# A two-layer DeltaNet and Conformer trunk: order of splits, filling, norm steps, scalar turns and first w_out columns

## The chip, the cores and the metric

One core of one Trainium2 chip runs the whole program. The metric is the device time of one execution in microseconds (us). Before the change three runs gave a median of 3172.94 us (3172.18 to 3173.76).

## What is computed

Two layers over 2048 tokens of width 1024, all in float32. Each layer normalises x, projects it, and has two branches: a gated DeltaNet (4 heads of 128, chunked scans forward and backward, summed) and a Conformer convolution (width 31, layer norm over 512 channels). Each branch is projected to 1024, the two are merged by sigmoid gates, and `w_out` follows.

```python
proj = h @ w_in                                   # 5648 columns: qkv, z_a, a, b, cf_val, cf_glu, z_b, gates
qkv = silu(depthwise_conv_centred(qkv, conv_w))   # width 5
g = -exp(a_log) * softplus(a_lg + dt_bias); beta = sigmoid(b_lg)
o = gated_delta_chunked(q, k, v, g[:, :, 0], beta[:, :, 0]) + flip(gated_delta_chunked(flipped inputs))
o = o * rsqrt(mean(o * o) + EPS) * dn_norm_w * silu(z_a);  y_a = o @ w_dn_out
u = depthwise_conv_centred(cf_val * sigmoid(cf_glu), cf_conv_w) + cf_conv_b
u = silu(layer_norm(u, cf_ln_w, cf_ln_b));                  y_b = (u * silu(z_b)) @ w_cf_out
gate = sigmoid(gate_lg + gate_b)
x = x + (gate[:, :, 0] * y_a + gate[:, :, 1] * y_b) @ w_out  # after the last layer: rms_norm
```

## The kernel before

Everything is kept channel by token, in 8 tiles of 128 channels; tokens come in halves of 1024 and blocks of 512. A float32 product is made of three matmuls: both operands are split into a high part (rounded to float32r by ScalarE, L158) and a low part (the difference, by VectorE, L159), and `dense_steps` (L170 to L178) issues high x high (L175), high x low (L176) and low x high (L177) for each 128 rows k of the contraction. A tile of one column of 128 outputs by 512 tokens is 24 matmuls for k = 8, or 12 for k = 4. `weight` (L161) loads a column of weights through SP and splits it; `whi`, `wlo` and `wraw` have two buffers each, `st` tiles three, `pd` banks of PSUM three and `pz` banks five.

The order of the work comes from generators. In the projections `dense` (L180) calls `follow` (one step of each of the queued head tasks in `post`) and `pump` (the background tasks in `back`) after each tile of matmuls; a background task yields its cost in us, and a yield of 0.0 ends this turn, so that the next step comes a tile later. `conformer_norm` (L749) is such a task for each of four blocks: mean (L766), squares and their token sum by `token_sum` (L201), reciprocal root on VectorE, `spread` over the channels (L212 on VectorE, L214 on TensorE), scale, SiLU, store of u on POOL's queue. The string `Z` says how many zero yields stand between the steps. `scalar_tiles` (L404) makes the 16 columns of decay and write strength per block (L414, L415), copies them (L417, into the `st` tile `ab`) and transposes them (L420); `scalars` (L424) is the first task in `post`, with the cumulative sums (L472 to L474). `conv_tiles` (L512) calls the block's scalar turn ahead of the block's two columns, and `step_lead` moves the norm of the coming block on.

`delta` (L818) is the scan: 16 steps, in each a forward and a backward chunk. All instructions from its start to the end of the filling are bound to the written order on TensorE, ScalarE, VectorE and GpSimd by `bind`. In a step, for both directions: products of k and of q with the state (L973, L976), `prep` of the coming chunks (L920 to L956), the inverse (L989), new state and output (L998, L1007), and `finish` of a pair of chunks: squares on ScalarE (L1028), reciprocal root on VectorE, scale on ScalarE (L1046), transposes (L1051) into `pz` and the product with the gate on VectorE (L1052), which is stored to `og` on SP. In between `pull(n)` takes n pieces of other TensorE work, a piece being the three matmuls of one k. LEAD says how many ahead of the first step, STEP how many at four places of each step, and TAIL how many ahead of each of the last five parts, of the last two pairs:

```python
            next(new)            # step: squares of the pair just finished
            pull(STEP[2])
            next(last)           # transposes of the pair before it
            ready = go(step + 1)
            last = new
            pull(STEP[3])
...
        for n, part in zip(TAIL, (new, last, new, new, new)):
            pull(n)
            next(part)
        for _ in fill:
            pass
        self.bind(start)
```

The pieces come from `filler` (L1135): 256 of `gates(1)`, then 64 of `early_merge` (L1171), which is the product of `w_cf` with u for the first half: 16 groups of four pieces, each with a sigmoid (L1181) at its start, a weight split at every other start, and the eviction y (L1187) at its end. u's eight splits are emitted when piece n of SPLITS has been taken and the next one is asked for.

`merge` (L1208) then does `w_dn` and (for the second half) `w_cf` for eight columns j, with gate loads and sigmoids (L1239), products (L1247, L1253, L1254), split into `yhi`, `ylo`; then the eight columns of `w_out`. In the last layer `last_out` (L1313) does this by blocks of 512 with a closing norm (`close`: token sums L206, spread, eight multiplies L1346, stores). Outside of the scan the scheduler of the tile framework places ready instructions by the order in which they were emitted.

Of the kernel before, what the change touches and what calls it, by code (L numbers as in the profile page):

```python
# [19 lines left out]
KD = 8  # L20
# [5 lines left out]
R1 = 3.0  # L26
R3 = 4.5
GAP = 0
SPLITS = (245, 247, 249, 251, 253, 255, 257, 258)
LEAD = (8, 10, 6, 6, 6, 4)  # L30
STEP = (4, 4, 4, 4)
TAIL = (2, 2, 1, 3, 4)
Z = '121'
PART = 5
LATE = 4
# [27 lines left out]
def cut(x):  # L63
    return x.rearrange("p (a i) -> p a i", a=2)
# [13 lines left out]
class Trunk:  # L78
# [325 lines left out]
    def scalar_tiles(self):  # L404
        nc = self.nc
        w = self.wab
        pt = self.pz()

        def block(blk):
            xs = self.hx(blk)  # L410
            ps = self.pd()
            for k in range(KD):
                xhi, xlo = (mix(x) for x in xs(k))
                nc.tensor.matmul(ps, w[:, k, :], xhi, start=k == 0, stop=False)  # L414
                nc.tensor.matmul(ps, w[:, k, :], xlo, start=False, stop=k == KD - 1)  # L415
            ab = self.st("ab")
            nc.scalar.activation(cut(ab[0:32, :]), sort(ps[0:32, :]), AF.Copy)  # L417
            for i in range(4):
                c = 4 * blk + i
                nc.tensor.transpose(pt[:, c * 32:(c + 1) * 32], ab[0:32, i * P:(i + 1) * P], self.ident[0:32, 0:32])  # L420

        return block, pt

    def scalars(self, pt):  # L424
        nc, l, a = self.nc, self.l, self.a
# [39 lines left out]
        v_.tensor_scalar(out=n(9), in0=n(9), scalar1=1.0, scalar2=None, op0=ALU.add)  # L465
        v_.reciprocal(out=n(9), in_=n(9))
        v_.tensor_copy(dch(self.beta), cdh(n(9)))
        yield
        ps = self.pz()
        tri = self.st("tri")[:, 0:256].rearrange("p (d c) -> p d c", d=2)  # L470
# [41 lines left out]
    def conv_tiles(self, cols, block=None):  # L512
        nc = self.nc
        self.rate = R1
        ws = [self.weight(self.a["w_in"][self.l, c], KD) for c in cols]
        accs = []
        prev = [None] * len(cols)
        for half in range(2):
            cur = []
            for i, c in enumerate(cols):  # L520
                cur.append(self.padded(half, TAPS, prev[i], "cin") if half or not i else None)
            for b in range(2):
                blk = 2 * half + b
                self.need(blk)
                if block:
                    self.step_lead(2)
                    block(blk)
                for i, c in enumerate(cols):
                    self.step_lead(2)
                    ps = self.pd()  # L530
                    self.dense(ps, ws[i], self.hx(blk), KD)
                    if cur[i] is None:
                        cur[i] = self.padded(half, TAPS, prev[i], "cin")
                    t, o = cur[i]
                    nc.scalar.activation(cut(t[:, o + b * NB:o + (b + 1) * NB]), sort(ps), AF.Copy)  # L535
            if half == 0 and self.l:
                self.need(2)
            for i, c in enumerate(cols):
                t, o = cur[i]
                prev[i] = t  # L540
                if half == 0:
                    accs.append(self.mid("acc"))
                n = HALF - 2 if half == 0 else HALF + 2
                out = accs[i][:, 0:n] if half == 0 else accs[i][:, HALF - 2:L]
                self.conv(out, t, n, TAPS, V_CONV + c * TAPS, 0.0)
                nc.scalar.activation(out, out, AF.Silu)
        self.rate = R2
        return accs
# [200 lines left out]
    def conformer_norm(self, blk):  # L749
        nc = self.nc  # L750
        v_ = nc.vector
        sl = slice(blk * NB, (blk + 1) * NB)
        cv = self.mid("lnc")[:, 0:L].rearrange("p (j t) -> p j t", t=NB)
        self.load(cv, self.cv_d[:, :, sl].rearrange("j p t -> p j t"))
        zb = self.mid("lnz")[:, 0:L].rearrange("p (j t) -> p j t", t=NB)
        self.load(zb, self.zb_d[:, :, sl].rearrange("j p t -> p j t"))
        t = self.st("lnt")
        s2 = self.st("lns")
        v_.tensor_tensor(out=t, in0=cv[:, 0, :], in1=cv[:, 1, :], op=ALU.add)
        v_.tensor_tensor(out=s2, in0=cv[:, 2, :], in1=cv[:, 3, :], op=ALU.add)  # L760
        v_.tensor_tensor(out=t, in0=t, in1=s2, op=ALU.add)
        yield 1.8
        for _ in range(int(Z[0])):
            yield 0.0
        ps = self.pz()
        nc.tensor.matmul(ps, self.ones, t, start=True, stop=True)  # L766
        v_.scalar_tensor_tensor(out=cv, in0=ps[:, None, :].to_broadcast([P, 4, NB]), scalar=-1.0 / 512,
                                in1=cv, op0=ALU.mult, op1=ALU.add)
        nc.scalar.activation(t, cv[:, 0, :], AF.Square)
        for j in range(1, 4):  # L770
            nc.scalar.activation(s2, cv[:, j, :], AF.Square)
            v_.tensor_tensor(out=t, in0=t, in1=s2, op=ALU.add)
        yield 4.0
        for _ in range(int(Z[1]) + (blk == 3)):
            yield 0.0
        pt = self.pz()
        self.token_sum(pt, t, 4)
        vv = self.sm(4, "lv")
        r = self.sm(4, "lr")
        v_.tensor_scalar(out=vv, in0=pt[:, 0:4], scalar1=1.0 / 512, scalar2=EPS, op0=ALU.mult, op1=ALU.add)  # L780
        self.rsqrt(r, vv, 4)
        yield 1.5
        for _ in range(int(Z[2])):
            yield 0.0
        pr = self.pz()
        self.spread(pr, r, 4)
        v_.tensor_tensor(out=cv, in0=cv, in1=pr[:, None, :].to_broadcast([P, 4, NB]), op=ALU.mult)
        yield 2.6
        for j in range(4):
            nc.scalar.activation(cv[:, j, :], cv[:, j, :], AF.Silu, scale=self.vec[:, V_LW + j:V_LW + j + 1],  # L790
                                 bias=self.vec[:, V_LATE + j:V_LATE + j + 1])
        v_.tensor_tensor(out=cv, in0=cv, in1=zb, op=ALU.mult)
        self.pstore(self.u_d[:, :, sl].rearrange("j p t -> p j t"), cv)
# [414 lines left out]
    def merge(self, l, xd, fnw):  # L1208
# [10 lines left out]
        for half in range(2):  # L1219
# [10 lines left out]
            for j in range(KD):  # L1230
                ys = {}
                wc = self.weight(a["w_cf"][l, j], 4) if half else None
                wd = self.weight(a["w_dn"][l, j], 4)
                for b in order:
                    tk = slice(half * HALF + b * NB, half * HALF + (b + 1) * NB)
                    gt = self.hm("gt")[:, 0:2 * NB].rearrange("p (n t) -> p n t", n=2)
                    n = 1 + half
                    self.load(gt[:, 0:n], self.gt_d.rearrange("(n j) p t -> j p n t", n=2)[j][:, 0:n, tk])
                    nc.scalar.activation(gt[:, 0:n], gt[:, 0:n], AF.Sigmoid)  # L1239
                    ys[b] = [gt[:, 0, :], gt[:, 1, :] if half else self.y1[:, j, b * NB:(b + 1) * NB]]  # L1240
                if half:
                    for b in order:
                        sl = slice(b * NB, (b + 1) * NB)
                        y = ys[b]
                        ps = self.pd()
                        self.dense(ps, wc, lambda k: (u[:, k, sl], u[:, 4 + k, sl]), 4)
                        v_.tensor_tensor(out=cut(y[1]), in0=sort(ps), in1=cut(y[1]), op=ALU.mult)  # L1247
                for b in order:
                    sl = slice(b * NB, (b + 1) * NB)
                    y = ys[b]  # L1250
                    ps = self.pd()
                    self.dense(ps, wd, lambda k: (og[:, k, sl], og[:, 4 + k, sl]), 4)
                    v_.tensor_tensor(out=cut(y[0]), in0=sort(ps), in1=cut(y[0]), op=ALU.mult)  # L1253
                    v_.tensor_tensor(out=y[0], in0=y[0], in1=y[1], op=ALU.add)  # L1254
                    self.split(yhi[:, j, sl], ylo[:, j, sl], y[0])
# [3 lines left out]
                og, pg = self.operands(self.og_d, 1, "gop")  # L1259
                ahead = (f(k) for f in (pu, pg) for k in range(4))  # L1260
            if last:
                self.last_out(l, half, xd, fnw, yhi, ylo, ahead, order)
                continue
            w = self.weight(a["w_out"][l, 0], KD)
            norm = self.normalise(0, *prev, wcol) if prev is not None else iter(())
            xn = []
            for j in range(KD):
# [42 lines left out]
        yield  # L1310
        yield from self.normalise(1, xn, r, wcol)

    def last_out(self, l, half, xd, fnw, yhi, ylo, ahead, order):  # L1313
        nc, a = self.nc, self.a
        v_ = nc.vector

# [39 lines left out]
        for b in order:  # L1356
# [1 line left out]
            xn = [t[:, i * NB:(i + 1) * NB] for t in (self.mid("xl"), self.mid("xl")) for i in range(4)]  # L1358
            ss = self.hm("ss")[:, 0:NB]
            whole = PART if half and b else KD  # L1360
            w = self.weight(a["w_out"][l, 0], KD)
            if whole < KD:
                hold = self.big([P, 2, KD, NB], F32R, "wend").rearrange("p a b c -> p (a b c)")
                parts = [hold[:, i * D:(i + 1) * D].rearrange("p (k c) -> p k c", c=P) for i in range(2 * (KD - whole))]
# [7 lines left out]
            for j in range(whole):  # L1372
# [7 lines left out]
                if whole < KD and j and len(ws) < KD - whole:  # L1380
# [2 lines left out]
                        self.split(hi[:, k:k + 4, :], lo[:, k:k + 4, :], raws[len(ws)][:, k:k + 4, :])  # L1383
                    ws.append((hi, lo))
            if whole == KD:
                run(close(o, NB, None))
                continue
            start = self.mark()
# [80 lines left out]
```

## Time and profile before

| | |
|---|---|
| median of 3 runs | 3172.94 us |
| the profiled execution | 3171.55 us |
| its span, first to last instruction | 3169.8 us |
| mean granted TensorE clock | 0.991 |
| busy: TensorE, VectorE, ScalarE, GpSimd | 3088.8, 2399.9, 1387.1, 298.9 us |

The profile is of one execution. PE is TensorE, DVE VectorE, ACT ScalarE, POOL GpSimd, SP SyncE (here a DMA queue). A line of a timeline gives the start, the duration, engine, line of the program, operation, written tile <- read tiles, shapes, how many such instructions were merged (x8), and in brackets how long the engine had been idle and which instruction ended that. Matmuls overlap: the distance of two starts, not the duration, is what one costs. PEclk is the granted clock as a share of 2.4 GHz; it has two levels, 0.5 (1.2 GHz) and 1.0, and a value between is a mix of both.

### The profile page before, as it was taken

To read this page: it belongs to the slowest core of one execution; us is meant where nothing else is said; L and a number is where in the kernel's file an instruction comes from. 1 tells how busy PE (TensorE), PEld (TensorE's weight loads), DVE (VectorE), ACT (ScalarE), POOL (GpSimd) and SP (SyncE) were. 2 spreads that over 40 slices of the span, in tenths; PEclk is the share of its full clock that TensorE was granted. 3 is DMA by queue.
4 is the path that set the end of the run, shared out by engine and by line. 5 is a ranking of instruction groups with operands and counts; after the bars stand their busy time and mean duration, and the time that the engine had idled before them with its cause. 6 is when DMAs were issued, how large, how long until landed. Compare 5 with 4: busy or idle time off the path is not lost. (4 is left out here: it accounts for less than half of the span.)

```text
span 3169.8 us, 51513 instructions
## 1 busy us (share of the span) xinstructions
PE 3088.8 (97%) x19190; PEld 2713.7 (86%) x19190; DVE 2399.9 (76%) x4441; ACT 1387.1 (44%) x3118; POOL 298.9 (9%) x297
## 2 busy tenths in 40 slices
PE   6999999999999999999999999999999999989998
PEld 5788888888889998888888888888888899878887
DVE  7789898997646698746676999999955567867665
ACT  5625252522344466533345252525233445655342
POOL 3000000000022222000000000000001213200000
PEclk9999999999999999999999999999999999999999
DMA  4232222233687786665413141414357878955643
GB/s 142 88 98 93 88 91 91 93 116 131 206 274 254 252 265 216 187 193 144 139 48 109 67 121 60 124 57 124 117 188 251 254 242 259 286 180 186 213 159 124
DMA packets 429420, 501.73 MB, mean 158 GB/s; under 512 B 96433, under 2 KB 262961, under 8 KB 429169
## 3 DMA queue, kind: packets, MB, share of 16 engines
q1 hardware_dynamic: 355840, 388.58, 39.5%
q10 hardware_dynamic: 65264, 80.09, 7.2%
q0 software_dynamic: 8064, 29.76, 2.5%
q8 instruction: 151, 2.47, 0.3%
q14 instruction: 101, 0.82, 0.1%
HBM read 342.74 MB, written 155.58 MB: 157 GB/s over the span
## 5 line engine op out<-in xcount | busy, mean ns | idle before, releaser
L175 PE MATMUL pd<-h,whi 128*128 128x512 f32 x2816 | 1092.2, 388 | 0.0
L177 PE MATMUL pd<-h,wlo 128*128 128x512 f32 x2816 | 1070.3, 380 | 1.4 <-DVE wlo L159 1.4
L176 PE MATMUL pd<-h,whi 128*128 128x512 f32 x2816 | 1071.3, 380 | 0.0
L734 DVE SCALAR_TENSOR_TENSOR cacc<-gp,vec,cacc 128x1009 f32<-128x1009 f32 (+1 forms) x480 | 614.9, 1281 | 29.1 <-ACT cacc L732 26.0
L175 PEld LDWEIGHTS pd<-h,whi 128*128 128x128 f32 x2816 | 534.1, 190 | 79.3 <-issue 1.4
L177 PEld LDWEIGHTS pd<-h,wlo 128*128 128x128 f32 x2816 | 533.8, 190 | 78.7 <-DVE wlo L159 2.2
L176 PEld LDWEIGHTS pd<-h,whi 128*128 128x128 f32 x2816 | 534.2, 190 | 72.5 <-issue 1.9
L158 ACT ACTIVATE whi<-wraw 128x512 fp32r<-128x512 f32 x394 | 239.4, 623 | 449.4 <-PE pd L176 327.9
L159 DVE TENSOR_TENSOR wlo<-wraw,whi 128x512 fp32r<-128x512 f32 x394 | 266.7, 690 | 114.4 <-ACT whi L158 113.7
L559 DVE SCALAR_TENSOR_TENSOR acc<-cin,vec,acc 128x1022 f32<-128x1022 f32 (+1 forms) x192 | 246.3, 1299 | 14.8 <-ACT acc L557 13.7
L177 PE MATMUL pd<-yhi,wlo 128*128 128x512 f32 x488 | 186.3, 382 | 4.6 <-DVE wlo L159 4.5
L175 PE MATMUL pd<-yhi,whi 128*128 128x512 f32 x488 | 186.4, 382 | 0.6 <-ACT whi L158 0.6
L176 PE MATMUL pd<-ylo,whi 128*128 128x512 f32 x488 | 185.6, 380 | 0.0
L814 ACT ACTIVATE go<-pd,vec 128x512 f32<-128x512 f32 x128 | 87.1, 680 | 141.2 <-PE pd L177 131.2
L746 ACT ACTIVATE ao<-pd 128x512 f32<-128x512 f32 x64 | 38.3, 598 | 193.7 <-PE pd L177 193.7
L535 ACT ACTIVATE cin<-pd 128x512 f32<-128x512 f32 x96 | 56.9, 593 | 150.0 <-PE pd L177 149.7
L175 PE MATMUL pd<-uop,whi 128*128 128x512 f32 x256 | 101.8, 398 | 9.6 <-ACT uop L158 9.6
L177 PEld LDWEIGHTS pd<-yhi,wlo 128*128 128x128 f32 x488 | 92.7, 190 | 20.1 <-DVE wlo L159 7.0
L175 PEld LDWEIGHTS pd<-yhi,whi 128*128 128x128 f32 x488 | 92.5, 190 | 14.8 <-ACT whi L158 2.0
L176 PEld LDWEIGHTS pd<-ylo,whi 128*128 128x128 f32 x488 | 92.7, 190 | 13.1
L176 PE MATMUL pd<-uop,whi 128*128 128x512 f32 x256 | 99.7, 390 | 0.5 <-DVE uop L159 0.5
L177 PE MATMUL pd<-uop,wlo 128*128 128x512 f32 x256 | 99.1, 387 | 0.0
(311 smaller groups left out, 4841.8 us busy)
## 6 DMA issues: line engine op xcount, KB each, us to landing
wraw<-w_in SPq DMA_DIRECT2D x240, 256.0 KB, 3.2
gt<-go ACTq DMA_DIRECT2D x128, 256.0 KB, 3.9
dl<-gr SPq DMA_DIRECT2D x128, 256.0 KB, 5.3
dl<-kq SPq DMA_DIRECT2D x64, 512.0 KB, 6.3
dl<-kv SPq DMA_DIRECT2D x64, 512.0 KB, 5.5
wraw<-w_out SPq DMA_DIRECT2D x90, 256.0 KB, 3.0
kq<-acc SPq DMA_DIRECT2D x16, 1024.0 KB, 5.3
gr<-go ACTq DMA_DIRECT2D x64, 256.0 KB, 2.2
```

The source lines that it names most:

```text
L158: self.nc.scalar.activation(hi, src, AF.Copy)
L159: self.nc.vector.tensor_tensor(out=lo, in0=src, in1=hi.bitcast(F32), op=ALU.subtract)
L175: mm(ps, whi[:, k, :], xhi, start=k == 0, stop=False)
L176: mm(ps, whi[:, k, :], xlo, start=False, stop=False)
L177: mm(ps, wlo[:, k, :], xhi, start=False, stop=k == kk - 1)
L535: nc.scalar.activation(cut(t[:, o + b * NB:o + (b + 1) * NB]), sort(ps), AF.Copy)
L559: self.nc.vector.scalar_tensor_tensor(out=out, in0=t[:, k:k + n], scalar=wc(k), in1=out, op0=ALU.mult, op1=ALU.add)
L734: self.nc.vector.scalar_tensor_tensor(out=acc, in0=t[:, k:k + n], scalar=wc(k), in1=acc, op0=ALU.mult, op1=ALU.add)
L746: nc.scalar.activation(cut(o), sort(ps), func)
L814: nc.scalar.activation(cut(o), sort(ps), AF.Identity, bias=self.vec[:, V_GB + j:V_GB + j + 1])
```

## The change

Five things are moved; no arithmetic is changed and none is added. SPLITS: u's eight splits are asked for after pieces 245, 247, 249 to 254. TAIL: four pieces instead of three ahead of the last pair's scale, eight instead of four ahead of its transposes. `conformer_norm`: one more zero yield ahead of block 2's token sum (block 3 had it) and one ahead of block 3's spread. `scalar_tiles` and `conv_tiles`: the block's transposes are issued behind the first column's matmuls; `scalars` has one yield more ahead of the cumulative sums. `merge` and `last_out`: the first `w_out` column is asked for during the last column j of the merge, and, for the second block of `last_out`, ahead of the first one's closing norm.

```diff
--- before.py
+++ after.py
@@ -26,10 +26,10 @@
 R1 = 3.0
 R3 = 4.5
 GAP = 0
-SPLITS = (245, 247, 249, 251, 253, 255, 257, 258)
+SPLITS = (245, 247, 249, 250, 251, 252, 253, 254)
 LEAD = (8, 10, 6, 6, 6, 4)
 STEP = (4, 4, 4, 4)
-TAIL = (2, 2, 1, 3, 4)
+TAIL = (2, 2, 1, 4, 8)
 Z = '121'
 PART = 5
 LATE = 4
@@ -415,9 +415,11 @@
                 nc.tensor.matmul(ps, w[:, k, :], xlo, start=False, stop=k == KD - 1)
             ab = self.st("ab")
             nc.scalar.activation(cut(ab[0:32, :]), sort(ps[0:32, :]), AF.Copy)
+            yield
             for i in range(4):
                 c = 4 * blk + i
                 nc.tensor.transpose(pt[:, c * 32:(c + 1) * 32], ab[0:32, i * P:(i + 1) * P], self.ident[0:32, 0:32])
+            yield
 
         return block, pt
 
@@ -466,6 +468,7 @@
         v_.reciprocal(out=n(9), in_=n(9))
         v_.tensor_copy(dch(self.beta), cdh(n(9)))
         yield
+        yield
         ps = self.pz()
         tri = self.st("tri")[:, 0:256].rearrange("p (d c) -> p d c", d=2)
         v_.tensor_scalar(out=tri, in0=self.con[:, C_MF:C_MB + 1, :], scalar1=0.0, scalar2=None, op0=ALU.is_equal)
@@ -524,11 +527,14 @@
                 self.need(blk)
                 if block:
                     self.step_lead(2)
-                    block(blk)
+                    turn = block(blk)
+                    next(turn)
                 for i, c in enumerate(cols):
                     self.step_lead(2)
                     ps = self.pd()
                     self.dense(ps, ws[i], self.hx(blk), KD)
+                    if block and i == 0:
+                        next(turn)
                     if cur[i] is None:
                         cur[i] = self.padded(half, TAPS, prev[i], "cin")
                     t, o = cur[i]
@@ -771,7 +777,7 @@
             nc.scalar.activation(s2, cv[:, j, :], AF.Square)
             v_.tensor_tensor(out=t, in0=t, in1=s2, op=ALU.add)
         yield 4.0
-        for _ in range(int(Z[1]) + (blk == 3)):
+        for _ in range(int(Z[1]) + (blk > 1)):
             yield 0.0
         pt = self.pz()
         self.token_sum(pt, t, 4)
@@ -780,7 +786,7 @@
         v_.tensor_scalar(out=vv, in0=pt[:, 0:4], scalar1=1.0 / 512, scalar2=EPS, op0=ALU.mult, op1=ALU.add)
         self.rsqrt(r, vv, 4)
         yield 1.5
-        for _ in range(int(Z[2])):
+        for _ in range(int(Z[2]) + (blk == 3)):
             yield 0.0
         pr = self.pz()
         self.spread(pr, r, 4)
@@ -1231,6 +1237,8 @@
                 ys = {}
                 wc = self.weight(a["w_cf"][l, j], 4) if half else None
                 wd = self.weight(a["w_dn"][l, j], 4)
+                if j == KD - 1 and not half:
+                    w0 = self.weight(a["w_out"][l, 0], KD)
                 for b in order:
                     tk = slice(half * HALF + b * NB, half * HALF + (b + 1) * NB)
                     gt = self.hm("gt")[:, 0:2 * NB].rearrange("p (n t) -> p n t", n=2)
@@ -1245,6 +1253,8 @@
                         ps = self.pd()
                         self.dense(ps, wc, lambda k: (u[:, k, sl], u[:, 4 + k, sl]), 4)
                         v_.tensor_tensor(out=cut(y[1]), in0=sort(ps), in1=cut(y[1]), op=ALU.mult)
+                if j == KD - 1 and half:
+                    w0 = self.weight(a["w_out"][l, 0], KD)
                 for b in order:
                     sl = slice(b * NB, (b + 1) * NB)
                     y = ys[b]
@@ -1259,9 +1269,9 @@
                 og, pg = self.operands(self.og_d, 1, "gop")
                 ahead = (f(k) for f in (pu, pg) for k in range(4))
             if last:
-                self.last_out(l, half, xd, fnw, yhi, ylo, ahead, order)
+                self.last_out(l, half, xd, fnw, yhi, ylo, ahead, order, w0)
                 continue
-            w = self.weight(a["w_out"][l, 0], KD)
+            w = w0
             norm = self.normalise(0, *prev, wcol) if prev is not None else iter(())
             xn = []
             for j in range(KD):
@@ -1310,7 +1320,7 @@
         yield
         yield from self.normalise(1, xn, r, wcol)
 
-    def last_out(self, l, half, xd, fnw, yhi, ylo, ahead, order):
+    def last_out(self, l, half, xd, fnw, yhi, ylo, ahead, order, w0):
         nc, a = self.nc, self.a
         v_ = nc.vector
 
@@ -1358,7 +1368,7 @@
             xn = [t[:, i * NB:(i + 1) * NB] for t in (self.mid("xl"), self.mid("xl")) for i in range(4)]
             ss = self.hm("ss")[:, 0:NB]
             whole = PART if half and b else KD
-            w = self.weight(a["w_out"][l, 0], KD)
+            w = w0
             if whole < KD:
                 hold = self.big([P, 2, KD, NB], F32R, "wend").rearrange("p a b c -> p (a b c)")
                 parts = [hold[:, i * D:(i + 1) * D].rearrange("p (k c) -> p k c", c=P) for i in range(2 * (KD - whole))]
@@ -1383,6 +1393,8 @@
                         self.split(hi[:, k:k + 4, :], lo[:, k:k + 4, :], raws[len(ws)][:, k:k + 4, :])
                     ws.append((hi, lo))
             if whole == KD:
+                if b == order[0]:
+                    w0 = self.weight(a["w_out"][l, 0], KD)
                 run(close(o, NB, None))
                 continue
             start = self.mark()
```

## Rows read from the trace of the kernel before

**Rows 1.** The page's first part: busy time, share, instructions of each engine.
```profile
PE 3088.8 (97%) x19190; PEld 2713.7 (86%) x19190; DVE 2399.9 (76%) x4441; ACT 1387.1 (44%) x3118; POOL 298.9 (9%) x297
```

**Rows 2.** Waits of TensorE, whole span: us in total, times, longest us.
```profile
PE pz L214 <- DVE dg L212: 14.9, 7, 3.5
...
PE pd L175 <- ACT uop L158: 9.6, 4, 3.4
PE pz L1051 <- ACT dm L1046: 6.7, 2, 3.9
PE pd L177 <- DVE wlo L159: 6.0, 5, 1.7
...
PE pz L420 <- ACT ab L417: 4.3, 2, 2.5
...
PE pz L472 <- DVE abw L462: 2.6, 2, 1.5
PE pz L201 <- DVE lnt L772: 2.5, 2, 1.9
```

**Rows 3.** Stretches: length, PE, PEld, DVE, ACT, POOL busy, PEclk, DMA, GB/s.
```profile
830.00:834.00 4.00, 3.15 (x13) 2.78 (x14) 2.49 (x13) 0.69 (x1) 0.00 (x0) 0.72 0.76 299
...
1234.00:1238.00 4.00, 4.00 (x15) 3.55 (x16) 3.71 (x7) 0.07 (x1) 0.00 (x0) 0.51 0.43 129
...
1284.00:1289.00 5.00, 4.83 (x14) 3.32 (x15) 2.56 (x5) 3.73 (x11) 0.00 (x0) 0.67 0.59 191
...
2414.00:2418.00 4.00, 3.50 (x14) 2.99 (x15) 3.28 (x6) 0.00 (x0) 0.00 (x0) 0.69 0.02 7
```

**Rows 4.** Timelines of TensorE and VectorE, layer 0, block 3's layer norm.
```profile
861.18 0.95 PE L201 MATMUL pz<-con,lnt 128*128 128x1 f32 x8
...
870.11 1.16 PE L214 MATMUL pz<-dg,con 128*128 128x128 f32 x8 [2.70 <-DVE dg L212]
...
869.77 0.87 DVE L212 TENSOR_SCALAR dg<-con,lr 128x128 f32<-128x128 f32 x4
```

**Rows 5.** Timeline of TensorE, layer 0, the first norm's last block.
```profile
90.64 1.74 PE L214 MATMUL pz<-dg,con 128*128 128x128 f32 x8 [2.00 <-DVE dg L212]
```

**Rows 6.** Timelines of TensorE and ScalarE, layer 0, the scan's last transposes.
```profile
1284.17 2.53 PE L1051 MATMUL pz<-con,dm 128*128 128x128 f32 x8 [2.76 <-ACT dm L1046]
...
1283.71 2.46 ACT L1046 ACTIVATE dm<-dm,orr 128x128 f32<-128x128 f32 x8 [2.68 <-DVE orr L1042]
```

**Rows 7.** Timelines of TensorE and ScalarE, layer 0, the first w_dn products.
```profile
1300.75 0.38 PE L175 MATMUL pd<-gop,whi 128*128 128x512 f32 x1
...
1301.39 0.38 PE L175 MATMUL pd<-gop,whi 128*128 128x512 f32 x1
...
1300.28 1.34 ACT L158 ACTIVATE gop<-gop 128x512 fp32r<-128x512 f32 x2 [1.43 <-DMA gop<-og]
```

**Rows 8.** Timeline of TensorE, layer 0, steps 13 and 14 of the scan.
```profile
1230.10 0.48 PE L175 MATMUL pd<-uop,whi 128*128 128x512 f32 x1 [3.42 <-ACT uop L158]
...
1238.76 1.06 PE L973 MATMUL pz<-dh,dl 128*128 128x128 f32 x8
```

**Rows 9.** Timeline of ScalarE, layer 0, same stretch.
```profile
1229.43 0.61 ACT L158 ACTIVATE uop<-uop 128x512 fp32r<-128x512 f32 x1
...
1230.58 1.28 ACT L1181 ACT_TABLE_LOAD   x1
1231.88 0.63 ACT L1181 ACTIVATE g<-g 128x512 f32<-128x512 f32 x1
```

**Rows 10.** Timeline of VectorE, layer 0, same stretch.
```profile
1219.89 1.29 DVE L159 TENSOR_TENSOR uop<-uop 128x512 fp32r<-128x512 f32 x2 [3.45 <-ACT uop L158]
...
1234.27 0.68 DVE L1187 TENSOR_TENSOR y<-pd,g 128x512 f32<-128x512 f32 x1
1234.87 1.40 DVE L1052 SCALAR_TENSOR_TENSOR dh<-pz,vec,dh 128x512 f32<-128x512 f32 x2
```

**Rows 11.** Timeline of VectorE, layer 1, first half's closing norm.
```profile
2941.63 5.36 DVE L1346 SCALAR_TENSOR_TENSOR xl<-xl,fnw,pz 128x512 f32<-128x512 f32 x8 [0.66 <-PE pz L214]
```

## The prediction

> **What bounds the kernel now.** The page's first part comes first: TensorE is busy for 97% of the span [rows 1]. So only its idle time, and time at its lower clock, can be won; the matmuls themselves stay. The view of the waits, filtered to TensorE, names that idle time [rows 2]: seven pairs that this change touches. The granted clock by stretches then shows that a wait costs more than itself: in the stretches behind a wait at 830, 1284 and 2414 us the clock reads 0.72, 0.67 and 0.69, between the levels 1.2 and 2.4 GHz, and it reads 0.51 after the two waits of the splits [rows 3]. I price one such lapse at 5.0 x (1 - 0.67) = 1.65 us, and that of the splits, two lapses long, at 3.3. Last the timelines of single engines, for who stands in whose queue.
>
> Durations are of the profiled execution: 3171.55 us, with a span of 3169.8. The median of the runs shown is 3172.94, 1.4 above it. A change of 0.2% (6.3 us) is about what a measurement of this kernel tells from none.
>
> **Layer norms a tile later.** An extra break in `conformer_norm` moves block 2's and block 3's token sums and block 3's spread back by one TensorE tile of 24 matmuls. Three matmuls (one k) take 0.64 us [rows 7], so a tile is 5.1 us. The waits removed are the token sums' (2.5 in two) and block 3's spreads': 2.70 in layer 0 [rows 4] and the longest of its pair, 3.5, in layer 1 [rows 2]. In block 3 the sum of 861.18 is followed by the spread's operands on VectorE only at 869.77 and later [rows 4], 8.6 to 9.5 us; two tiles give 10.2, so the cover suffices by about 0.7. With the two lapses beside them: 2.5 + 2.7 + 3.5 + 3.3 = 12.0 us. It adds no instruction. Block 3 now ends two tiles later, and its store of u, on POOL's queue, runs into the first loads of the scan on SP; the scan's first 40 pieces of filling (26 us) hide it. Bounds: 8.7 (waits only) to 12.0.
>
> **Scalar turns later.** The four transposes of a block now follow the first column's 24 matmuls. The wait on ScalarE's copy is 4.3, in two [rows 2]. The 2.5 of layer 0 I don't count: 9 us later TensorE waits 2.00 at a spread for VectorE [rows 5], and that moment comes from the chain of the first norm, so TensorE would only arrive there sooner. Layer 1's 1.8 stays won. The extra break in `scalars` covers both waits for the cumulative sums, 2.6. Against it: `ab` keeps one of three `st` buffers for a tile more, which can hold up the squares of the first norm; no row shows that, so between 0 and 3 lost; I take 1, since the buffer is otherwise free at most turns. Sum 1.8 + 2.6 - 1 = 3.4 (1.4 to 6.9).
>
> **More filling before the last transposes.** Five more pieces stand ahead of them, 5 x 0.64 = 3.2 us per layer. The waits are 6.7, the longest 3.9 [rows 2]. The scale on ScalarE starts at 1283.71 and paces the transposes, which take 2.53 [rows 6]; none of this gets faster. What is won is that five pieces no longer lie behind the transposes, 3.2, and the lapse, 1.65: 4.9 per layer. What is late next: the first `w_dn` products need `gop`, loaded from what these transposes write. Its last split ends about 1302.3 (ACT, then VectorE) against a first product at 1300.75 [rows 7]; the second block's k = 3 is wanted 12 + 9 matmuls, 4.5 us, after that, at 1305.3. Slack 3.0; TensorE comes 4.9 earlier, so up to 1.9 returns as a wait. SP's gate loads and the extra evictions (`y`) now precede the final eviction on VectorE, but the final products' own loads hold that back anyway. I take the middle, 3.9 per layer: 7.8 (6.0 to 9.8).
>
> **Splits before the squares.** Removed per layer: 3.42 at the product of 1230.10 [rows 8] and the rest of the pair's 9.6 in four [rows 2], with the DVE part 5.0, and 3.3 of clock: 8.3. But TensorE is then early for something else. The program has five `pz` banks. At step 14, the second direction's products of `k` and state (L973) take the bank of the first transposed output (L1051), free once VectorE's L1052 has read it. L1052 stands behind `y` (L1187), `y` behind the first sigmoid, the sigmoid behind the table load, the weight split and the eight squares. Now count. The two splits more in the earlier group cost VectorE 1.3 ahead of the state [rows 10], which passes to the squares; the split at 1229.43 goes away, 0.6 [rows 9]. So the sigmoid of 1231.88 starts at about 1232.5 and ends at 1233.15; `y` takes 0.68 and the first L1052 0.70 [rows 10]: bank free at 1234.55. TensorE, ready at 1230.10 - 3.42 = 1226.68, does three pieces (1.9) and 16 matmuls of 128 columns (2.1) and stands there at 1230.7. New wait: 3.9. Before, the same L973 started at 1238.76 [rows 8]: 4.2 us sooner. The clock will lapse after the new wait, as after the old ones, and this lapse lies behind the point compared, while the old one was over by then: 1.65 to 3.3 off. Left 0.9 to 2.6; I take 2.0, for one lapse and some, per layer: 4.0. Full bounds 0 to 16.6 (no bank wait at all).
>
> The table load took 1.28 us, and the sigmoid followed 0.02 after its end [rows 9]. The Trainium skill, "ScalarE: Activation LUTs", section "What ACT_TABLE_LOAD costs", says every switch costs a drain of about 1.38 us besides; if a drain fell due behind the shorter queue, an estimate by that page would make the new wait 5.3 and the gain 0.6 per layer. No such gap stands in this row, so the sum goes by the row.
>
> **w_out sooner.** Six first columns are asked for earlier, two loads each on SP, ahead of gate loads or of the closing norm. The waits for `wlo` (6.0 with others [rows 2]) aren't at first columns: the one in layer 1's first half is the third column's, whose subtraction stands behind the eight multiplies begun at 2941.63 [rows 11]; the split of the next first column is done before those already. Term 0; between -3 (SP and ACT held by an early split that waits for a weight buffer) and +5.
>
> **Sum.** 12.0 + 3.4 + 7.8 + 4.0 + 0 = 27.2; 3171.55 - 27.2 = 3144.4, on the median's footing 3145.7, said as 3145.5.
>
> **The rivals.**
>
> *No bank wait* (the splits' whole 16.6 is won, if the buffers are handed out otherwise or VectorE is sooner): 12.6 better, 3133. For it: no such wait is in the rows now. Against: five banks counted by name. Chance 0.17.
>
> *The cover behind the scan runs out* (og's store, load and split come late by more than 1.9, the clock lapses at the first `w_dn` products): the tail's 7.8 and the splits' 4.0 are given back: 3157.5. For it: 3.0 of slack against 4.9. Chance 0.14.
>
> *The parts outside the written order don't do what they say*: the scheduler puts layer norms and transposes where they were. Then only 7.8 + 4.0 remain: 3161. Against it: the steps of the norms stand a tile apart in the trace as written. Chance 0.06.
>
> *Slower: the held `ab` buffer.* At eight turns (four per layer) the squares or the next h wait for a buffer up to a tile, 5.1: 41 us lost at most, 27 won, 3187. It decides once eight turns lose over 3.4 each. Against it: the transposes' wait itself is in two turns of eight. Chance 0.04.
>
> **How the numbers follow.** The forecast has 0.59, with its own range 3139 to 3152 from the bounds of the terms together. To leave out no more than 2 in 10, the range reaches to the first two rivals: 3131 to 3158. Faster: all but the slow rival and what of the third and of unforeseen stalls ends near zero: 0.91. Within 0.2%: 0.05. Slower: 0.04.
>
> **What would show it.** Right: no TensorE wait on `lnt` or block 3's `dg` before the scan; `uop` waits gone, and in their place about 4 us at L973 ended by L1052 in step 14 of both layers, with a clock near 0.6 after it; `dm` waits under 1.5 in all; up to 2 us at `gop`; the `wlo` waits unchanged. Wrong: no wait at L973 (first rival), a long one at `gop` (second), L201 of `lnt` still two tiles behind L766 for block 2 (third), or new waits for `sqa` or `h` at the start of a layer (fourth).

## The result: 0.18% slower, and the profile after

The changed kernel took 3177.2 us (median of 22 runs, 3171.1 to 3185.8) against 3173.0 for the kernel before beside it: a ratio of 1.0018 with an interval of 1.0012 to 1.0024. The forecast was 3145.5, and 3131 at the low end to 3158 at the high end. The profiled execution has a span of 3176.0 us, 6.2 longer than before.

The page's first part (busy time, share and instructions of each engine) answers to [rows 1], and the view of TensorE's waits (us in total, times, longest) to [rows 2]:

```profile
PE 3087.8 (97%) x19190; PEld 2715.3 (85%) x19190; DVE 2400.1 (76%) x4441; ACT 1382.5 (44%) x3113; POOL 298.4 (9%) x297
```

```profile
PE pz L573 <- ACT acc L552: 14.9, 2, 8.3
...
PE pz L214 <- DVE dg L212: 9.6, 6, 3.3
PE pd L177 <- DVE wlo L159: 9.4, 7, 1.9
PE pz L979 <- DVE dh L1058: 8.5, 2, 4.2
...
PE pd L175 <- ACT dm L1052: 3.2, 2, 1.8
PE pz L421 <- ACT ab L417: 2.5, 1, 2.5
...
PE pz L475 <- DVE abw L464: 2.2, 2, 1.2
```

TensorE is busy as long as before; only what lies between its work has changed. Of the pairs of [rows 2], `uop` and `lnt` are gone, `dg` and `ab` are smaller, and the wait at the `k` products of step 14 (L979, L973 before) has come as forecast. The last transposes' wait for `dm` is gone too; the line that still names `dm` is that of another product, read below. The first line is the surprise: the transposes of a head's convolved channels (L573, `token_major`) wait for `acc`, which ScalarE's SiLU ends (L552). No wait of that kind stood in the kernel before. The timeline of TensorE shows it in layer 0, with a wait for a weight right behind it, and in the last line in layer 1:

```profile
276.25 1.12 PE L573 MATMUL pz<-con,acc 128*128 128x128 f32 x4 [8.30 <-ACT acc L552]
...
281.83 0.80 PE L177 MATMUL pd<-h,wlo 128*128 128x512 f32 x1 [1.90 <-DVE wlo L159]
...
1828.78 0.48 PE L573 MATMUL pz<-con,acc 128*128 128x128 f32 x1 [6.57 <-ACT acc L552]
```

To see what each stage lost, I added up over stretches of 2 us TensorE's idle time and its busy time times (1 - granted clock). The last column is an experiment below, the change without its extra yield.

| stage, us lost to waits and clock | before | after | without the yield |
|---|---|---|---|
| 0 to 120: first norm, scalar turns | 37.7 | 33.2 | 33.9 |
| 200 to 320 and 1780 to 1900: head 1 begins | 1.4 | 27.1 | 1.4 |
| 760 to 940 and 2300 to 2490: layer norms | 12.3 | 5.0 | 11.2 |
| 1150 to 1248 and 2700 to 2800: splits | 16.0 | 12.7 | 13.2 |
| 1248 to 1420 and 2800 to 2880: behind the scan | 10.1 | 3.9 | 2.8 |
| the whole span | 101.5 | 109.6 | 88.6 |

Four stages of the forecast gave 21.3 us (4.5 + 7.3 + 3.3 + 6.2). One that the forecast never looked at took 25.7: of its 27.1 after the change, 18.7 were idle time and 8.4 the clock. (The start of the second half's merge, 1420 to 1460, lost 3.3 more; the sums are rough, 8.1 in all against 6.2 of span.)

**What is late there.** The stretches of VectorE tell it (columns as in [rows 3]). First the kernel before, then the changed one:

```profile
205.00:225.00 20.00, 20.00 (x94) 17.50 (x94) 19.80 (x35) 3.45 (x6) 0.57 (x1) 1.00 0.30 110
...
265.00:285.00 20.00, 20.00 (x100) 17.57 (x100) 19.96 (x18) 11.11 (x25) 0.00 (x0) 1.00 0.28 81
```

```profile
205.00:225.00 20.00, 20.00 (x95) 17.44 (x94) 3.04 (x6) 6.37 (x10) 1.13 (x2) 1.00 0.23 80
...
265.00:285.00 20.00, 9.80 (x42) 8.05 (x41) 20.00 (x30) 12.22 (x45) 0.00 (x0) 0.65 0.44 121
```

VectorE, the third pair of numbers, is full in both stretches before. After the change it does 3.04 us in the first 20, and TensorE, with its clock at 0.65 on average, 9.80 in the second. In the kernel before, eleven taps of the convolution (L734, 1.26 us each) start in the first stretch, with the short steps of the first triangular solve between them. In the changed kernel these taps are done by 201.8 us and the solve has not begun: its first transpose on TensorE comes 52 us later. Kernel before, then changed kernel, timeline of TensorE:

```profile
171.91 0.27 PE L660 MATMUL pz<-con,bh 128*32 128x128 f32 x1
```

```profile
224.17 0.27 PE L666 MATMUL pz<-con,bh 128*32 128x128 f32 x1
```

The code says why. `post` holds head 0's `scalars`, `keys` and `values`, one step per tile. With the extra yield in `scalars`, the last step of `keys` no longer comes on the last tile ahead of `back.append(conformer_conv(0, 0))` but on the first behind it, and that last step is what appends `solve(0)`. So the background queue `back` holds the convolution first and the solve second. Two things follow on VectorE. The short operations that end `keys` (L191 to L197, 0.17 us each) now stand between convolution taps of 1.27 us. In the kernel before, the timeline of VectorE reads

```profile
157.78 0.17 DVE L609 TENSOR_SCALAR ssq<-ssq 128x16 f32<-128x16 f32 x1 [4.67 <-ACT junk L605]
...
162.22 0.20 DVE L636 TENSOR_TENSOR bh<-beta,rk 128x32 f32<-128x32 f32 x1
```

and in the changed one

```profile
157.38 0.17 DVE L615 TENSOR_SCALAR ssq<-ssq 128x16 f32<-128x16 f32 x1
157.50 1.27 DVE L740 SCALAR_TENSOR_TENSOR cacc<-gp,vec,cacc 128x1009 f32<-128x1009 f32 x1
158.69 0.17 DVE L191 TENSOR_SCALAR rq<-ssq 128x16 int32<-128x16 int32 x1
...
175.09 0.22 DVE L642 TENSOR_TENSOR bh<-beta,rk 128x32 f32<-128x32 f32 x1
```

4.4 us became 17.7. And the solve, which begins with a round trip through memory, begins when the convolution that had covered that trip is used up. Its last elimination step on VectorE ends at 294.49 instead of 241.59, and until then its steps and the next convolution's taps stand between those of head 1's own convolution (L565), whose end `acc` waits for.

### The profile page after: what moved, and what is told of

It reads as the page before. It is cut to its first block, busy times and chain, and to the rows that moved or that the text cites. A ratio compares the mean times of both kernels' runs of the same rounds, so it can differ in the third digit from the quotient of the medians.

```text
span 3176.0 us, 51511 instructions
## 1 busy us (share of the span) xinstructions
PE 3087.8 (97%) x19190; PEld 2715.3 (85%) x19190; DVE 2400.1 (76%) x4441; ACT 1382.5 (44%) x3113; POOL 298.4 (9%) x297
## 5 line engine op out<-in xcount | busy, mean ns | idle before, releaser
L565 DVE SCALAR_TENSOR_TENSOR acc<-cin,vec,acc 128x1022 f32<-128x1022 f32 (+1 forms) x192 | 245.7, 1299 | 11.5 <-ACT acc L563 10.5
L175 PEld LDWEIGHTS pd<-yhi,whi 128*128 128x128 f32 x488 | 92.2, 189 | 15.7 <-ACT whi L158 3.0
```

The source lines that it names most:

```text
L175: mm(ps, whi[:, k, :], xhi, start=k == 0, stop=False)
L565: self.nc.vector.scalar_tensor_tensor(out=out, in0=t[:, k:k + n], scalar=wc(k), in1=out, op0=ALU.mult, op1=ALU.add)
```

## The experiments

Ratios are to the kernel before on the same chip, with their 95% intervals; 0.001 is 3.2 us. Executions of one kernel spread over some 10 us here, so differences under 0.002 between two kernels are not settled. Without the yield, line numbers behind it are one lower (L978 for L979).

**The yield alone, both ways.** Theory: the queue's order, as above. Rival: the loss lies at the new bank wait or behind the scan.

```diff
         v_.tensor_copy(dch(self.beta), cdh(n(9)))
         yield
-        yield
```

> The change without the extra yield in scalars; the rest stays. Theory (queue order): the yield lets the last step of head 0's keys come after the first conformer convolution has been queued, so that the first triangular solve stands behind it in the background queue, and TensorE waits 8.3 and 6.6 us for an acc with a long lapse of the clock after it. Matched instructions put this at 14.5 us in layer 0 and 11.7 in layer 1. Then this run takes 3177.2 - 26.2 = 3151 us (3147 to 3155), with no wait at the transposes of acc. Rival (the loss lies elsewhere, at the bank wait of step 14 and behind the scan): no change, 3175 to 3178.

Measured: 0.9939 (0.9922 to 0.9956), 3156.9 us, no wait for `acc`. The kernel before with only that yield:

> The kernel before with the extra yield in scalars alone. Theory (queue order): 3173 + 26 = 3199 us (3193 to 3204), with waits near 8 and 6 us at the transposes of acc. Rival (loss elsewhere): 3170 to 3174, the 2.6 us of waits for the cumulative sums won.

Measured: 1.0090 (1.0073 to 1.0106), 3203.2 us, with waits of 15.7 in two at the transposes of `acc`. Both runs agree: the yield costs 0.0079 to 0.0090, 25 to 29 us. It wins next to nothing: the waits for the cumulative sums, 2.6 in two [rows 2], are 2.2 in two in the changed kernel, 2.1 in two without the yield, and 1.6 in one with the yield alone.

**How it does so.** If it is the order of the two background tasks, putting the solve in front must be enough:

```diff
-        self.back.append(self.solve(hd, bh))
+        (self.back.append if hd else self.back.appendleft)(self.solve(hd, bh))
```

> The whole change, yield included, but the solve of head 0 is put at the front of the background queue instead of its end. Theory (queue order): the order of the kernel before is restored and VectorE has convolution work during the loads of the solve; 3151 us (3147 to 3156), no wait at the transposes of acc. Rival (the key steps are a tile late in themselves, whatever the background queue holds): 3174 to 3178 and the waits of 8.3 and 6.6 us stay.

Measured: 1.0017 (1.0007 to 1.0027). The wait for `acc` is gone as the theory had it, and the time is that of the rival. TensorE now waits for weights: over the whole span 24.9 us for `wlo`, where the changed kernel has 9.4. The view of its waits from 200 to 250 us of this kernel has one line.

```profile
PE pd L177 <- DVE wlo L159: 9.3, 2, 6.0
```

The theory as first put fell. The next run keeps the yield but takes one step out of head 0's `keys`, so that their end is back on its tile:

```diff
-        yield from self.token_major(kt, k_out, (0, 2))
+        yield from self.token_major(kt, k_out, (0, 2) if hd else (1,))
```

> The whole change with its extra yield in scalars, but one yield less in head 0's keys (two transposes of k in one step of eight, where two steps were). The scalars' sums stay a tile later; the end of the keys, and with it the first triangular solve, is back on the tile where the kernel before had it. Theory (the solve's start, a tile late, runs VectorE out of other work in a stage where it is full): no wait at the transposes of acc and a ratio to the kernel before near 0.994 (0.992 to 0.997), some 3152 to 3160 us. Rival (the later cumulative sums themselves do the harm): 1.001 to 1.003.

Measured: 0.9945 (0.9928 to 0.9962), 3159.2 us, no wait for `acc`, and VectorE is full again (third pair of numbers):

```profile
205.00:225.00 20.00, 20.00 (x94) 17.52 (x93) 19.71 (x37) 3.45 (x6) 0.57 (x1) 1.00 0.30 105
```

So it is the tile on which the keys end, not the scalars' sums. Three more runs, all without the yield, split that up: the order of the two tasks alone, the solve a tile late in the right order, and the values a tile late.

```diff
-            self.back.append(self.conformer_conv(j, half, t))
+            (self.back.append if j or half else self.back.appendleft)(self.conformer_conv(j, half, t))
```

> The change without the extra yield, but the first conformer convolution is put in front of head 0's solve in the background queue; the keys end on the tile where the kernel before ends them. Theory A (it is the order of the two tasks: with the solve behind the convolution, VectorE has nothing beside the solve's loads): as in the whole change, a wait of some 8 and 6 us for an acc and a ratio of 1.000 to 1.003. Theory B (it is the keys' end a tile late in itself): 0.994.

Measured: 0.9987 (0.9977 to 0.9998): between the two theories, with an interval apart from that of the changed kernel and from that without the yield. 0.0048 of the 0.0079 is the order alone. VectorE empties in the same stretch, and the wait for `acc` is 3.7 us, not 8.3:

```profile
205.00:225.00 20.00, 20.00 (x94) 17.42 (x94) 5.91 (x14) 2.60 (x5) 1.09 (x2) 1.00 0.32 106
```

```diff
         yield 3.0
         yield 0.0
+        if hd == 0:
+            yield 0.0
```

> The change without the extra yield, the queue's order kept, but head 0's solve starts one tile later by a zero yield of its own. Theory A' (the solve's start has no tile of slack, in whatever order): waits for wlo near 9 us as with the solve put first, a ratio of 0.999 to 1.003. Rival (a tile's delay is harmless as long as the order is kept, and the run with the solve put first lost for another reason, such as the keys' and values' own steps): 0.993 to 0.996.

Measured: 0.9934 (0.9914 to 0.9954). Its first transpose comes 5 us later (173.94 against 168.98), and that does no harm while the convolution is not ahead of it.

```diff
+        if hd == 0:
+            yield
         yield from self.token_major(vt, v_out)
```

> The change without the extra yield, and head 0's values one step later by a yield of their own; the keys end, and the solve and the convolution are queued, as in the kernel before. Theory V (what is left beside the queue's order is the values' transposes and evictions a tile late): a ratio of 0.998 to 1.003 with new waits for wlo or acc between 200 and 300 us. Theory K (only the keys' end counts, by what it queues and when): 0.993 to 0.995 and no such wait.

Measured: 0.9933 (0.9916 to 0.9950): harmless too. What remains beside the order, 0.0031, goes with the keys' own end behind the convolution's start. That the taps between its short operations are this remainder fits the timeline of the changed kernel, but not the run with the solve put first, where they ran in one piece (`bh` at 161.02) and the loss came as weight splits queued behind taps and solve. How that part works is not settled.

**The forecast's other terms, each taken out of the kernel without the yield (0.9939).** How well 0.9939 holds is seen in three kernels that came out equal to it: the solve late (0.9934), the values late (0.9933), `w_out` as before (0.9933, below). SPLITS as before:

> The change without the extra yield and with SPLITS as before. Matched instructions give the splits 1.9 and 2.5 us over the scan: 3151 + 4.4 = 3155.5 (3153 to 3158), the waits of 3.4 and 1.2 us for uop back and no wait at L979. Rival (the bank wait gives back everything): the same as without the yield alone, within 1 us.

Measured: 0.9962 (0.9948 to 0.9976), with the waits for `uop` back (8.9 in four) and none at the `k` products of step 14: SPLITS are worth 0.0023, some 7 us. TAIL as before:

> The change without the extra yield, TAIL as before: fewer pieces ahead of the last scale and transposes. Forecast's term (3.9 us per layer, 7.8 in all): 0.9939 + 0.0025, a ratio of 0.9964 (0.9955 to 0.997), with waits of 2.8 and 3.9 us at the last transposes. Rival (the loads of gop behind the scan take it back): 0.994 to 0.9948.

Measured: 0.9954 (0.9941 to 0.9966), with waits of 7.6 us in two at the last transposes: 0.0015, some 5 us, between the forecast's term and the rival and too small to be settled by itself. The stage behind the scan lost 10.9 us in this run against 2.8 without the yield (2.5 to 7.6 in the others with TAIL moved), so the forecast's 7.8 is not ruled out either. The norms' breaks as before:

> The change without the extra yield, the layer norms' breaks as before. Theory (the breaks only moved the wait to block 2's spread; TensorE's idle time and clock in that stage are 12.3 us before and 11.8 without the yield): 0.0000 to 0.0006 above 0.9939. Rival (the forecast's term of 12.0 us): 0.9939 + 0.0038, a ratio of 0.9977.

Measured: 0.9968 (0.9957 to 0.9980): 0.0029, some 9 us, much nearer to the forecast's term than to mine by then. The stage of the layer norms lost 16.7 us in this run against 11.2 with the breaks and 12.3 in the kernel before: what the breaks are worth depends on how the norms fall between the weight splits. The transposes of the scalar turns as before:

> The change without the extra yield, and the scalar transposes where the kernel before has them, behind the squares' copy at once. The forecast's term without the yield's 2.6 is 1.8 less 1 for the held buffer: 0.8 us, a ratio of 0.994 (0.9935 to 0.9945) with the wait of 1.8 us for ab back. Rival (the turns also shorten the first norm's stage, which lost 3.8 us less of idle time and clock in the run without the yield): 0.995 to 0.996.

Measured: 0.9961 (0.9947 to 0.9975): 0.0022, some 7 us, above both, and the interval still takes in the rival. The first columns of `w_out` as before:

> The change without the extra yield and without the earlier first column of w_out. Matched instructions of the run without the yield lose some 3 us against the kernel before over the second half's merge of layer 0. Theory (the earlier loads and splits of w_out stand in front of the gate loads): 2 to 4 us less than without the yield alone, a ratio of 0.993 (0.991 to 0.994). Rival (w_out's place costs and gives nothing, as forecast): the same as without the yield alone, 0.994.

Measured: 0.9933 (0.9918 to 0.9949): the rival; nothing to be seen of a cost. Added up, the four terms come to 0.0089, more than the 0.0061 that the kernel without the yield wins: they are not independent, or each carries noise of its own.

**Two repairs.** The layer norms' wait had moved to block 2's spread. In the kernel without the yield the timeline of TensorE shows it, and that of VectorE what holds it: a weight split stands in the middle of the reciprocal root and waits 5.45 us for ScalarE.

```profile
840.96 0.80 PE L214 MATMUL pz<-dg,con 128*128 128x128 f32 x2 [3.86 <-DVE dg L212]
```

```profile
832.13 0.16 DVE L193 TENSOR_SCALAR rsv<-lv 128x4 f32<-128x4 f32 x1
837.75 0.69 DVE L159 TENSOR_TENSOR wlo<-wraw,whi 128x512 fp32r<-128x512 f32 x1 [5.45 <-ACT whi L158]
838.35 0.15 DVE L195 TENSOR_TENSOR rst<-lr,rsv 128x4 f32<-128x4 f32 x1
...
840.62 0.87 DVE L212 TENSOR_SCALAR dg<-con,lr 128x128 f32<-128x128 f32 x4
```

```diff
-        for _ in range(int(Z[2]) + (blk == 3)):
+        for _ in range(int(Z[2]) + (blk > 1)):
             yield 0.0
```

> The change without the extra yield, and block 2's spread put one tile later too (block 3's had it already). Theory (the forecast took the layer norms' waits as gone, but the wait moved to block 2's spread, where VectorE's root stands behind a weight split): waits of 3.9 and 2.9 us and a lapse of some 3 us go, so 7 to 10 us less than without the yield alone: a ratio of 0.991 (0.990 to 0.993). Rival (the next step of the norm is late in its place, block 3's token sum or its spread): the same as without the yield, 0.994.

Measured: 0.9914 (0.9895 to 0.9933), 3147.7 us; no wait at a spread between 770 and 900 us, and the layer norms' stage lost 1.6 us. The second repair is for the bank wait of step 14. In the changed kernel the products of the second direction wait for VectorE's L1058, which stands behind the eviction `y`, which waits for the sigmoid behind the squares and the table load (timelines of TensorE, VectorE and ScalarE):

```profile
1238.92 2.08 PE L979 MATMUL pz<-dh,dl 128*128 128x128 f32 x8 [4.23 <-DVE dh L1058]
...
1237.52 0.69 DVE L1193 TENSOR_TENSOR y<-pd,g 128x512 f32<-128x512 f32 x1 [1.25 <-ACT g L1187]
1238.12 1.40 DVE L1058 SCALAR_TENSOR_TENSOR dh<-pz,vec,dh 128x512 f32<-128x512 f32 x2
...
1235.56 1.28 ACT L1187 ACT_TABLE_LOAD   x1
1236.86 1.15 ACT L1187 ACTIVATE g<-g 128x512 f32<-128x512 f32 x2
```

```diff
-            nc.scalar.activation(g, g, AF.Sigmoid)
+            if i:
+                nc.scalar.activation(g, g, AF.Sigmoid)
...
+            if n == SPLITS[-1]:
+                self.nc.scalar.activation(gs[0], gs[0], AF.Sigmoid)
```

> The change without the extra yield, and the first gate's sigmoid emitted right after u's last split, in front of ScalarE's eight squares (it was behind them). Theory (the wait of 4.2 us for a pz bank comes from VectorE's eviction y, which waits for that sigmoid): the wait at the second direction's products of step 14 falls from 4.2 to under 1 in both layers, and with the clock 8 to 13 us less than without the yield alone: a ratio of 0.991 (0.9895 to 0.9925). Rival (the table load now in front delays the squares and what follows them, or the bank is late for another reason): the same as without the yield, 0.994.

Measured: 0.9920 (0.9905 to 0.9935), 3151.0 us. The wait fell from 4.2 to 2.45, not under 1: the next bank's owner, ScalarE's scale of the state products, stands behind the same squares.

```profile
1229.30 0.94 PE L978 MATMUL pz<-dh,dl 128*128 128x128 f32 x6 [2.45 <-ACT dm L987]
```

Both repairs together, and the same with `w_out` as before:

> Both repairs together: without the extra yield, block 2's spread a tile later, the first sigmoid in front of the squares. If they are independent, as their stages are 400 us apart: 0.9939 - 0.0025 - 0.0019, a ratio of 0.9895 (0.988 to 0.991). Rival (what TensorE gains early it waits for at the next step that has its own pace): not below 0.9914, the better of the two alone.

> The same two repairs, and the first columns of w_out asked for where the kernel before did. Theory (the earlier w_out costs 2 to 4 us): 0.0006 to 0.0012 below the kernel with both repairs. Rival (it costs nothing): equal to it within 0.0005.

Measured: 0.9910 (0.9897 to 0.9923), 3146.2 us, and 0.9910 (0.9895 to 0.9924), 3146.4 us. They beat the kernel before by 0.9%, but the two repairs do not add up: beside block 2's spread the sigmoid brings nothing that can be told. The stage sums (one profiled execution each) show where it went. Without block 2's spread and with it, moving the sigmoid takes the splits' stage from 13.2 to 8.2 and from 12.6 to 8.6, and raises what is lost behind the scan from 2.8 to 7.2 and from 4.9 to 8.5. By these sums most of the gain came back as a loss behind the scan, as the rival had it; but the other kernels that have TAIL moved and the sigmoid in its place lose 2.5 to 7.6 there, so this is a pointer and not a proof. And `w_out` is worth nothing that these runs can tell, either way.

## Why the prediction was wrong

**The step that failed** is a half sentence in the scalar turns: "The extra break in `scalars` covers both waits for the cumulative sums, 2.6." It neither covered them (2.2 left of 2.6) nor was it asked what is queued behind it. In its place the runs showed this: a yield in a task of `post` moves every later step of that queue by a tile, up to the step that appends a task to another queue, and this one passed the place where the convolution is appended. It cost 25 us where 2.6 were credited. I had looked for the harm of this part at the `ab` buffer; that rival gave the right sign for the wrong reason: in the changed kernel the waits for `sqa` are 14.7 where 17.5 stood before, and those for `h` 8.2 where 7.2 stood. The outcome lies in what the forecast called within 0.2%, at a chance of 0.05.

Without that line the forecast would have said 24.6 us won; the kernel without the yield won 0.0061, 19 us (14 to 25). **Term by term:**

- *Layer norms, 12.0.* 7.3 in the changed kernel's stage, some 9 by the run with the breaks taken out, both below it. The cover was counted for block 3 only. Block 2's sum was moved and its spread not: 2.51 is left at block 2's spread of layer 1 in the changed kernel, and 3.86 and 2.90 at block 2's spreads in the kernel without the yield. The missing break was the repair that showed most.
- *Splits, 4.0.* Right in mechanism and place: a wait at L979 for a bank behind L1058, 4.23 us against the 3.9 worked out. The stages lost 3.3 us less, the run says some 7.
- *The table load.* The sigmoid of the changed kernel follows the load 0.02 us after its end (1235.56 + 1.28, then 1236.86), as it did before [rows 9]. The drain of about 1.38 us that the Trainium skill, "ScalarE: Activation LUTs", section "What ACT_TABLE_LOAD costs", adds to a switch does not show here either.
- *Behind the scan, 7.8.* 6.2 by the stages, some 5 by the run with TAIL as before. The transposes no longer wait for `dm`. What waits, 3.2 in two, is a `w_cf` product one piece ahead of them. The profile names the scale (`dm`), but the product reads `u` and weights only; it is the first of its group of four pieces and needs a `pd` bank, of which there are three, and that of three groups earlier is freed by the eviction `y` that ends at 1287.48, 0.14 us before it starts (2840.80 and 2840.95 in layer 1). This `y` stands on VectorE right behind the last reciprocal root. That is read from the program and these times, no run tests it; if it holds, it is the kind of bank wait that the forecast counted at step 14 and did not look for here. The first `w_dn` products wait 0.4 for `y` and 0.2 for `gop`, less than the 1.9 allowed. TensorE and VectorE in the changed kernel:

```profile
1287.62 0.45 PE L175 MATMUL pd<-uop,whi 128*128 128x512 f32 x1 [1.37 <-ACT dm L1052]
...
1288.45 1.28 PE L1057 MATMUL pz<-con,dm 128*128 128x128 f32 x8
...
1286.70 0.17 DVE L1048 TENSOR_TENSOR orr<-orr,cq 128x8 f32<-128x8 f32 x1
1286.79 0.69 DVE L1193 TENSOR_TENSOR y<-pd,g 128x512 f32<-128x512 f32 x1
```

- *Turns, 0.8 without the yield.* The run says some 7 us, which the forecast had too small, and layer 0 went another way than its working. Layer 1's wait for `ab` is gone as counted: the transposes come 5.49 us behind the block's last product. In layer 0 they stand where they stood, as the third rival had it (5.15 us behind that product in both kernels, at the block that waits), and the wait of 2.5 stayed; what went is the spread's 2.00 [rows 5], which the forecast had as fixed, and most of a 2.38 at a token sum (0.43 is left). Both are back in the run with the turns as before. But the 2.00 is gone in the run with the yield alone too, where the turns are not moved, so what removes it is open. Before, then after:

```profile
81.68 0.43 PE L420 MATMUL pz<-con,ab 32*128 32x32 f32 x4 [2.50 <-ACT ab L417]
```

```profile
78.53 0.43 PE L421 MATMUL pz<-con,ab 32*128 32x32 f32 x4 [2.51 <-ACT ab L417]
...
88.20 1.05 PE L214 MATMUL pz<-dg,con 128*128 128x128 f32 x8
```

- *w_out, 0.* Nothing else was measured, to within some 5 us.

Of the signs named beforehand the bank wait came true in both layers (8.5 in two), with a clock of 0.62 and 0.53 in the two stretches of 4 us from 1236 in layer 0, and 0.68 and 0.90 in those from 2792 in layer 1. The gone `lnt`, `uop` and block 3's `dg` came true, and so did that for `dm` at the transposes, though not for the pieces ahead of them. None was named for the stage that lost, and the waits for `wlo` did not stay unchanged. They grew from 6.0 to 9.4, not by `w_out` but by the two of 1.9 behind the waits for `acc`.

## What to carry to other kernels

A yield in a cooperative schedule is not a local delay: list every step that is queued behind it and every queue that those steps append to, and see whether one of them passes another task on the way. Where an engine is nearly full for 100 us (VectorE was busy for 95.9 of the 100 us from 205 to 305 in the kernel before), a task that starts with a round trip through memory must be started ahead of the bulk work that covers it; here the order alone was worth 0.0048. And when a step of a chain is moved later, look at the step after it too, or the wait only changes its name. Where a profile names a releaser that the waiting instruction does not read, look for the buffer that it writes.

## What the runs showed of the hardware

Idleness of an engine off the critical path was not free: VectorE did 16.8 us less in the stretch of 205 to 225 us, and TensorE lost 14.4 us more between 200 and 320. The two are not in a fixed ratio: with the convolution put first, VectorE did 5.91 us in that stretch, 13.9 less than before, and TensorE lost 5.5 more. The clock made the long wait dearer: in the 20 us around the wait of 8.3 us its mean was 0.65, as low as the 4 or 5 us behind the shorter waits of [rows 3], and in the 4 us from 276, right behind the wait, it was 0.50, the lower of its two levels.
